# Gate and up projections of a decoder trunk by one level of Strassen's algorithm

## The chip, the cores and the metric

The kernel runs on one NeuronCore of a Trainium2 chip, which has a matrix engine (TensorE, PE in the rows; PEld is its weight load), three engines for elementwise work (VectorE = DVE, ScalarE = ACT, GpSimd = POOL) and a queue for loads (SyncE = SP). The metric is the device time of one execution, in microseconds (us), and the median over runs.

## What is computed

Two layers, each a half-weighted SwiGLU feed-forward, a mixer of three attentions, and a second feed-forward, on 512 tokens of width 1024. The change touches the feed-forwards alone: four of them, with 2816 hidden columns.

```python
def swiglu(h, w_gate, w_up, w_down):
    return (jax.nn.silu(h @ w_gate) * (h @ w_up)) @ w_down

for layer in range(DEPTH):                       # DEPTH = 2
    x = x + 0.5 * swiglu(rmsnorm(x, norm_g[layer, 0]), ffn_w_gate[layer, 0], ffn_w_up[layer, 0], ffn_w_down[layer, 0])
    x = x + hybrid_mixer(rmsnorm(x, norm_g[layer, 1]), ...)
    x = x + 0.5 * swiglu(rmsnorm(x, norm_g[layer, 2]), ffn_w_gate[layer, 1], ffn_w_up[layer, 1], ffn_w_down[layer, 1])
```

## The kernel before

Everything is float32. x lies transposed: the 1024 channels on the partitions in 8 chunks of 128, the 512 tokens along the columns. Each operand of a product is split into a high part (ScalarE copies it into the matrix engine's rounded float32) and a low part (VectorE subtracts the high part), and `mm3` makes one product of three matrix instructions: high by low, high by high, low by high. The norm's gain is applied before the products, 1/rms per token (`n.rb`, broadcast over the partitions) afterwards.

A feed-forward goes through its 22 hidden chunks of 128 in three parts (`FF_PARTS`: 8, 8 and 6 chunks). For each chunk `f`, two weight tiles of 128x1024 (gate and up) are loaded on SP's queue and split by `load_w`; 8 products for gate go into a bank of PSUM, 8 for up into another, 512 columns each, 48 matrix instructions in all. `activated` then makes silu(gate) * up: VectorE scales the gate by `rb`, ScalarE takes silu, GpSimd scales by `rb` once more, VectorE multiplies by up, and the result is split again into `h` and `lo`. When a part's chunks are done, its share of the down projection follows: 8 chunks of x, each with one weight tile and 3 instructions per hidden chunk, added to x.

The buffers that matter: `RAW = 4` raw weight tiles, `HL = 4` high and low parts of them, three banks each with the tags `sc` and `tr` and two with `mm`. A scheduler sets the order of instructions on every engine when the program is built; each engine then works through its own list strictly in that order and waits on semaphores where an operand isn't ready. Within the matrix engine's list the chunks of a part follow one another.

Of the kernel before, what the change touches and what calls it, by code (L numbers as in the profile page):

```python
# [22 lines left out]
T = 512          # tokens  # L23
NT = T // P      # token tiles
D = 1024
KD = D // P      # chunks of the model width
DFF = 2816
NF = DFF // P    # chunks of the feed-forward width
# [3 lines left out]
TOPK = 128       # min(256, 512 // 4)  # L32
NEG = -1e30
TAKEN = -3e38
WCOLS = 1024     # columns of one weight tile
SLOTS = 35       # buffers of [P, 512] for hidden chunks, x, heads and outputs
T1 = 3           # buffers by tag
# [4 lines left out]
RAW = 4  # L42
HL = 4
BANKS = {"mm": 2, "sc": 3, "tr": 3}
WARM = 9         # products of zeros at the start
# attention beside the dense products, counted in steps of six of these
RATE = 1         # units of attention per step
PICKS = 0.36     # rounds of the top-k per step
LAG_I, LAG_N = 4, 7             # from a projection to the split of its heads, without and with their norm
LAG_S, LAG_H = 4, 3             # to the norm's scaling; from the split to the transposes  # L50
LAG_T, LAG_C, LAG_V = 3, 5, 2   # from the softmax to the transposes (C: with both its maps), to the values
AHEAD = 4        # gates of branch a that come before its attention's end
FF_PARTS = [(0, 8), (8, 8), (16, 6)]
# [5 lines left out]
# columns of w_in, as the reference splits them  # L59
# [16 lines left out]
def trunk_kernel(ctx, tc, xt_in, pos_in, ng_in, wgu, wdn, wgrp, wgate, wbr_s, wbr_c, wo, qkg_in, lam_in, subg_in, out):  # L76
# [6 lines left out]
    tmp = ctx.enter_context(tc.tile_pool(name="tmp", bufs=2))  # L83
    sm = ctx.enter_context(tc.tile_pool(name="sm", bufs=3))
# [12 lines left out]
    def slot(dt=F32, tag="h", cols=512):  # L97
        return big.tile([P, cols], dt, tag=tag, name=nm(tag), bufs={"h": SLOTS, "xs": 16}[tag])

    def temp(tag, dt=F32, cols=512, bufs=2):  # L100
        return tmp.tile([P, cols], dt, tag=tag, name=nm(tag), bufs=bufs)

    # products of zeros, while the first loads are under way, bring the array's clock up
# [19 lines left out]
    causal = const.tile([P, 512], BF16, name="causal")   # last 128 columns: 0 on and below the diagonal  # L123
# [170 lines left out]
    def ffn(l, half, n, nxt, aside=None, x_src=None):  # L294
        for pi, (f0, nf) in enumerate(FF_PARTS):
            hh, hl = [], []
            late = []
            for f in range(f0, f0 + nf):
# [4 lines left out]
                if first:  # L303
                    for c in range(1, KD):
                        n.chunk(c, x_from(x_src, c), False)
# [572 lines left out]
```

## Time and profile before

| | |
|---|---|
| median of 3 runs | 2357.59 us (2356.71 to 2360.36) |
| profiled execution: span from first to last instruction | 2354.5 us |
| what lies around the span, by the median | 3.1 us |
| PE busy | 2338.9 us, 99% of the span |
| DVE, ACT, POOL busy | 1251.1, 897.3, 476.8 us |
| granted TensorE clock, mean | 0.999 |

The span is what the trace shows; the profiled execution's own device time is not listed apart from it, so the runs' median stands beside it. The page's busy time of an engine counts the time in which it had work in hand, so 99% for PE says that it hardly ever had none, not that each product runs at its best. The other engines' idle time costs nothing as long as PE doesn't wait for them.

### The profile page before, as it was taken

The numbers are of one execution on the slowest core, as the hardware profiler recorded it, in microseconds if no ns is written. First come the engines' busy times: TensorE is split into PE (matmuls) and PEld (weight loads), VectorE is DVE, ScalarE is ACT, GpSimd is POOL, SyncE is SP. The second block draws the span as 40 slices with busy tenths as digits, with TensorE's granted clock in tenths as the row PEclk, the third lists the DMA queues.
The fourth block names the chain that finished last, engine by engine and source line by source line (L and its number), as shares of the span: only waits on it lengthen the run. The fifth ranks groups of instructions, "written<-read, shape, count | busy, mean of one in ns | idle before, by whom it ended". The sixth has DMA issues, their size and how long they took to land.

```text
span 2354.5 us, 29137 instructions
## 1 busy us (share of the span) xinstructions
PE 2338.9 (99%) x11077; PEld 1939.2 (82%) x11077; DVE 1251.1 (53%) x2244; ACT 897.3 (38%) x1634; POOL 476.8 (20%) x495
## 2 busy tenths in 40 slices
PE   9999999999999999999999999999999999999999
PEld 7888888888888888888888888888888888888887
DVE  5434344788865543333443343447889665433333
ACT  4322234666534432222332222346755343322221
POOL 3101013454111310110220110134641112101010
PEclk9999999999999999999999999999999999999999
DMA  5333333323222333333333333332322223333332
GB/s 170 110 99 99 96 97 99 104 79 93 81 94 81 129 96 99 97 94 95 98 101 93 95 99 99 108 112 78 95 77 81 91 85 125 99 98 99 99 92 69
DMA packets 71290, 229.64 MB, mean 98 GB/s; under 512 B 8688, under 2 KB 8688, under 8 KB 71152
## 3 DMA queue, kind: packets, MB, share of 16 engines
q1 hardware_dynamic: 70432, 227.12, 31.2%
q8 instruction: 87, 1.43, 0.2%
q10 hardware_dynamic: 720, 0.68, 0.1%
q14 instruction: 51, 0.42, 0.1%
HBM read 214.13 MB, written 6.29 MB: 94 GB/s over the span
## 4 chain that ended last, share of the span: by engine, by line
PE 93%; DVE 3%; DMA 1%; POOL 1%; issue 1%; ACT 0%; SPq 0%; POOLq 0%; ACTq 0%; DVEq 0%
PE mm L214 18%; PE mm L216 17%; PE mm L215 17%; PE sc L214 8%; PE sc L215 8%; PE sc L216 8%; PE mm L364 4%; PE mm L365 4%; PE mm L366 4%; DMA h<-h 1%; PE sc L453 1%; PE sc L454 1%; PE tr L476 1%; PE tr L435 1%; PE tr L501 1%
## 5 line engine op out<-in xcount | busy, mean ns | idle before, releaser
L208 ACT ACTIVATE hi<-raw 128x1024 fp32r<-128x1024 f32 (+3 forms) x410 | 421.8, 1030 | 1118.6 <-PE mm L215 719.2
L209 DVE TENSOR_TENSOR lo<-raw,hi 128x1024 fp32r<-128x1024 f32 (+3 forms) x410 | 500.6, 1222 | 74.5 <-ACT hi L208 73.5
L214 PE MATMUL mm<-xs,hi 128*128 128x512 f32 x1088 | 431.2, 396 | 1.2 <-DVE xs L232 1.2
L216 PE MATMUL mm<-xs,lo 128*128 128x512 f32 x1088 | 425.0, 391 | 0.0
L215 PE MATMUL mm<-xs,hi 128*128 128x512 f32 x1088 | 424.9, 390 | 0.0
L282 POOL TENSOR_TENSOR t<-t,rb 128x512 f32<-128x512 f32 x88 | 149.2, 1696 | 1110.9 <-ACT t L281 1110.9
L214 PE MATMUL mm<-h,hi 128*128 128x512 f32 x832 | 324.1, 390 | 0.5 <-DVE h L805 0.5
L216 PE MATMUL mm<-h,lo 128*128 128x512 f32 x832 | 323.7, 389 | 0.0
L215 PE MATMUL mm<-h,hi 128*128 128x512 f32 x832 | 323.7, 389 | 0.0
L214 PE MATMUL sc<-xs,hi 128*128 128x512 f32 x704 | 274.7, 390 | 1.3 <-ACT hi L208 1.3
L216 PE MATMUL sc<-xs,lo 128*128 128x512 f32 x704 | 274.3, 390 | 0.0
L215 PE MATMUL sc<-xs,hi 128*128 128x512 f32 x704 | 274.1, 389 | 0.0
L214 PEld LDWEIGHTS mm<-xs,hi 128*128 128x128 f32 x1088 | 204.6, 188 | 44.1 <-issue 2.4
L216 PEld LDWEIGHTS mm<-xs,lo 128*128 128x128 f32 x1088 | 204.7, 188 | 43.1
L215 PEld LDWEIGHTS mm<-xs,hi 128*128 128x128 f32 x1088 | 205.0, 188 | 39.0
L284 DVE TENSOR_TENSOR t<-sc,t 128x512 f32<-128x512 f32 x88 | 60.9, 692 | 286.6 <-PE sc L216 277.2
L329 DVE SCALAR_TENSOR_TENSOR h<-mm,h 128x512 f32<-128x512 f32 x96 | 66.4, 692 | 264.1 <-PE mm L216 264.1
L214 PEld LDWEIGHTS mm<-h,hi 128*128 128x128 f32 x832 | 156.2, 188 | 34.2 <-DVE h L805 2.0
L215 PEld LDWEIGHTS mm<-h,hi 128*128 128x128 f32 x832 | 156.2, 188 | 32.4
L216 PEld LDWEIGHTS mm<-h,lo 128*128 128x128 f32 x832 | 156.2, 188 | 32.3
L279 DVE TENSOR_TENSOR t<-mm,rb 128x512 f32<-128x512 f32 x88 | 60.7, 691 | 220.8 <-PE mm L216 220.8
L364 PE MATMUL mm<-hi,xs 128*128 128x512 f32 (+2 forms) x448 | 172.3, 385 | 0.0
(293 smaller groups left out, 3166.7 us busy)
## 6 DMA issues: line engine op xcount, KB each, us to landing
raw<-in_wgu SPq DMA_DIRECT2D x174, 512.0 KB, 3.6
raw<-in_wdn SPq DMA_DIRECT2D x64, 512.0 KB, 3.5
raw<-in_wgate SPq DMA_DIRECT2D x48, 512.0 KB, 3.6
raw<-in_wgrp SPq DMA_DIRECT2D x40, 512.0 KB, 3.6
raw<-in_wdn SPq DMA_DIRECT2D x32, 384.0 KB, 3.1
raw<-in_wo SPq DMA_DIRECT2D x16, 512.0 KB, 3.5
h<-h SPq DMA_DIRECT2D x56, 128.0 KB, 4.4
aside<-h SPq DMA_DIRECT2D x16, 256.0 KB, 2.0
```

The source lines that it names most:

```text
L208: S.activation(hi[:, sl], raw[:, sl], AF.Copy)
L209: V.tensor_tensor(lo[:, sl], raw[:, sl], hi[:, sl].bitcast(F32), op=ALU.subtract)
L214: PE.matmul(o, ah, bl, start=first, stop=False)
L215: PE.matmul(o, ah, bh, start=False, stop=False)
L216: return PE.matmul(o, al, bh, start=False, stop=last)
L279: V.tensor_tensor(g, pg, n.rb, op=ALU.mult)
L282: G.tensor_tensor(s, s, n.rb, op=ALU.mult)
L284: V.tensor_tensor(hf, pu, s, op=ALU.mult)
L329: V.scalar_tensor_tensor(x[d], o, 0.5, x[d], op0=ALU.mult, op1=ALU.add)
L364: PE.matmul(o[:, :w_cols], xl, wh[:, sl], start=k == 0, stop=False)
L365: PE.matmul(o[:, :w_cols], xh, wh[:, sl], start=False, stop=False)
L366: last_dense[0] = PE.matmul(o[:, :w_cols], xh, wl[:, sl], start=False, stop=k == KD - 1)
```

## The change

Tokens are halved into a left and a right half of 256 columns, the model chunks into even and odd ones, and the outputs of a chunk into gate and up. The eight half-size products of these halves (2 by 2 by 2) become seven, by one level of Strassen's algorithm in a form with 15 sums. In short:

- **x** (`fold`): for each pair of an even and an odd chunk, VectorE, GpSimd and ScalarE make the halves, their sums and differences, and both parts of each, 256 columns wide. This happens when x is finished (at the start, or as the stage before ends).
- **weights** (`folded_w`): two raw tiles `r0`, `r1` per hidden chunk. The two parts of `r0` as before, 1024 wide (weights 1 and 2). GpSimd makes four sums, 128x512 each: `s1`, `s3` in new buffers (`SUMS = 3`), two in place over raw halves. Then ScalarE and VectorE split five tiles of 128x512 (`shi`, `slo`; `SHL = 5`) for weights 6, 5, 7, 3 and 4.
- **products** (`gate_up`): seven products of 4 x 3 matrix instructions, 256 columns each, in the order 1, 2, 6, 5, 7, 3, 4, on two banks: the left half of one (`sc`, called `q`) gathers products 1, 6, 7, 4, the other (`tr`, called `o`) 2, 5, 3. In between, ScalarE copies what `q` holds after product 1 and after product 6 (the two halves of `e`, below eL and eR), and what `o` holds on the right after product 5 (`u`); VectorE adds to `u` after product 7, and `o` to `e` after product 3. A product that goes on in `q` waits for the copy or sum that reads it.
- **`activated`**: as before, with the two halves of `hf` made apart, and with -1/rms (`nrb`) on GpSimd.
- parts of 6, 6, 5 and 5 chunks in place of 8, 8 and 6; one pool of 48 buffers in place of 35 and 16; a pool per stage, for the tiles that only one stage needs; a new layout of the gate and up weights.

The diff, cut to its core:

```diff
-SLOTS = 35
+SLOTS = 48
+SUMS = 3
+SHL = 5
-FF_PARTS = [(0, 8), (8, 8), (16, 6)]
+FF_PARTS = [(0, 6), (6, 6), (12, 5), (17, 5)]
+H2 = T // 2
+Q4 = KD // 2
...
+        def fold(self, c, xc):
+            g = ng[:, self.idx * KD + c:self.idx * KD + c + 1]
+            L, R = slice(0, H2), slice(H2, T)
+            if c % 2 == 0:
+                bh, bl = slot(F32R), slot(F32R)
+                y = temp("t2")
+                V.tensor_scalar(y, xc, g, None, op0=ALU.mult)
+                d = temp("t0", cols=H2)
+                S.activation(bh[:, L], y[:, L], AF.Copy)
+                G.tensor_tensor(d, y[:, L], y[:, R], op=ALU.subtract)
+                V.tensor_tensor(bl[:, L], y[:, L], bh[:, L].bitcast(F32), op=ALU.subtract)
+                S.activation(bh[:, R], d, AF.Copy)
+                V.tensor_tensor(bl[:, R], d, bh[:, R].bitcast(F32), op=ALU.subtract)
...
+                return
+            y, d = self.even
+            ah, al = slot(F32R), slot(F32R)
+            S.activation(ah, xc, AF.Copy, scale=g)
+            V.scalar_tensor_tensor(al, xc, g, ah.bitcast(F32), op0=ALU.mult, op1=ALU.subtract)
...
+            V.scalar_tensor_tensor(f[:, R], xc[:, R], g, d, op0=ALU.mult, op1=ALU.add)
+            V.scalar_tensor_tensor(f[:, L], xc[:, R], g, y[:, R], op0=ALU.mult, op1=ALU.subtract)
...
+            S.activation(ch[:, R], f[:, R], AF.Copy, scale=-1.0)
+            V.scalar_tensor_tensor(cl[:, R], f[:, R], -1.0, ch[:, R].bitcast(F32), op0=ALU.mult, op1=ALU.subtract)
+            S.activation(ch[:, L], f[:, L], AF.Copy)
+            V.tensor_tensor(cl[:, L], f[:, L], ch[:, L].bitcast(F32), op=ALU.subtract)
...
+            V.scalar_tensor_tensor(q, xc[:, L], g, f[:, R], op0=ALU.mult, op1=ALU.subtract)
+            S.activation(dh, q, AF.Copy, scale=-1.0)
+            V.scalar_tensor_tensor(dl, q, -1.0, dh.bitcast(F32), op0=ALU.mult, op1=ALU.subtract)
...
+    def folded_w(src, pieces=1):
+        r0, r1 = (wp.tile([P, WCOLS], F32, tag="raw", name=nm("raw"), bufs=RAW) for _ in range(2))
+        L, R = slice(0, 512), slice(512, 1024)
+        h0, l0 = (wp.tile([P, WCOLS], F32R, tag=t, name=nm(t), bufs=HL) for t in ("hi", "lo"))
...
+            nc.sync.dma_start(r0, src[0])
+            S.activation(h0, r0, AF.Copy)
+            V.tensor_tensor(l0, r0, h0.bitcast(F32), op=ALU.subtract)
+        nc.sync.dma_start(r1, src[1])
+        pool = phase[-1]
+        s1, s3 = (pool.tile([P, 512], F32, tag="sum", name=nm("sum"), bufs=SUMS) for _ in range(2))
+        G.tensor_tensor(s1, r1[:, L], r1[:, R], op=ALU.add)
+        G.tensor_tensor(s3, r0[:, R], r1[:, L], op=ALU.add)
+        G.tensor_tensor(r1[:, L], r0[:, R], s1, op=ALU.add)
+        G.tensor_tensor(r0[:, R], r0[:, L], r1[:, L], op=ALU.add)
+        w = {1: (h0[:, R], l0[:, R]), 2: (h0[:, L], l0[:, L])}
+        for j, t in ((6, r1[:, L]), (5, s1), (7, s3), (3, r0[:, R]), (4, r1[:, R])):
+            h, lo = (pool.tile([P, 512], F32R, tag=x, name=nm(x), bufs=SHL) for x in ("shi", "slo"))
+            S.activation(h, t, AF.Copy)
+            V.tensor_tensor(lo, t, h.bitcast(F32), op=ALU.subtract)
+            w[j] = h, lo
+        return w
+
+    def gate_up(n, w, after):
+        q, o = bank("sc"), bank("tr")
+        L, R = slice(0, H2), slice(H2, T)
+        def product(j, to, first):
+            for i in range(Q4):
+                (ah, al), (bh, bl) = (x[:, i * P:(i + 1) * P] for x in w[j]), n.ops[j][i]
+                mm = mm3(to, ah, al, bh, bl, first and i == 0, i == Q4 - 1, not first)
+            after(mm)
+        e = temp("e")
+        product(1, q[:, L], True)
+        product(2, o[:, L], True)
+        S.activation(e[:, L], q[:, L], AF.Copy)
+        product(6, q[:, L], False)
+        product(5, o[:, R], True)
+        S.activation(e[:, R], q[:, L], AF.Copy)
+        u = temp("u", cols=H2)
+        S.activation(u, o[:, R], AF.Copy)
+        product(7, q[:, L], False)
+        product(3, o[:, R], False)
+        V.tensor_tensor(u, q[:, L], u, op=ALU.add)
+        V.tensor_tensor(e, e, o, op=ALU.add)
+        product(4, q[:, L], False)
+        return e, q[:, L], u
+
+    def activated(n, e, q, u):
+        L, R = slice(0, H2), slice(H2, T)
+        V.tensor_tensor(e, e, n.rb, op=ALU.mult)
         s = temp("t1", bufs=T1)
-        S.activation(s, g, AF.Silu)
-        G.tensor_tensor(s, s, n.rb, op=ALU.mult)
+        S.activation(s, e, AF.Silu)
+        G.tensor_tensor(s, s, n.nrb, op=ALU.mult)
         hf = temp("t2")
-        V.tensor_tensor(hf, pu, s, op=ALU.mult)
+        V.tensor_tensor(hf[:, L], q, s[:, L], op=ALU.mult)
+        V.tensor_tensor(hf[:, R], u, s[:, R], op=ALU.mult)
...
-                ws = [load_w(wgu[l, half, f, j], WCOLS, 2 if first else 1) for j in range(2)]
+                w = folded_w(wgu[l, half, f], 2 if first else 1)
...
+                late.append(gate_up(n, w, n.advance))
```

How the order moves, at three places of the first feed-forward, in the middle of a part. First ACT's list. Before, in the part's fourth to sixth chunk (L208 is the high part of a raw tile, L281 silu, L286 the high part of the result):

```order
L208 ACTIVATE hi_657<-raw_656 128x1024
L281 ACTIVATE t_107_574<-t_106_572 128x512
L208 ACTIVATE hi_663<-raw_662 128x1024
L286 ACTIVATE h_579<-t_108_577 128x512
L208 ACTIVATE hi_730<-raw_729 128x1024
L281 ACTIVATE t_120_647<-t_119_645 128x512
L208 ACTIVATE hi_736<-raw_735 128x1024
L286 ACTIVATE h_652<-t_121_650 128x512
```

And of the change, around its second part's second chunk, whose banks are `sc_1553` and `tr_1554` (the first one's are 1415 and 1416; L392 is eL, L416 the high part `h` of the chunk before, L360 the 1024-wide high part h0 of the part's fourth chunk, L372 the high parts of the third chunk's folded weights, L395 eR, L397 the copy u):

```order
L392 ACTIVATE e_1555<-sc_1553 128x256
L416 ACTIVATE h_1515<-t_272_1512 128x512
L360 ACTIVATE hi_1797<-raw_1795 128x1024
L372 ACTIVATE shi_1671<-raw_1658 128x512
L395 ACTIVATE e_1555<-sc_1553 128x256
L372 ACTIVATE shi_1675<-sum_1665 128x512
L397 ACTIVATE u_1606<-tr_1554 128x256
L372 ACTIVATE shi_1679<-sum_1666 128x512
L372 ACTIVATE shi_1683<-raw_1657 128x512
L372 ACTIVATE shi_1687<-raw_1658 128x512
```

Two high parts and two steps of the activation a chunk have become three copies out of PSUM, six high parts and two steps, and the copies stand between them: eR behind `h`, h0 and a `shi`. Next DVE's list. Before (L279 and L284 multiply out of PSUM, L209 is a low part, L287 the result's):

```order
L279 TENSOR_TENSOR t_106_572<-mm_522,rb_340 128x512
L209 TENSOR_TENSOR lo_658<-raw_656,hi_657 128x1024
L284 TENSOR_TENSOR t_108_577<-sc_523,t_107_574 128x512
L209 TENSOR_TENSOR lo_664<-raw_662,hi_663 128x1024
L287 TENSOR_TENSOR h_580<-t_108_577,h_579 128x512
L279 TENSOR_TENSOR t_119_645<-mm_595,rb_340 128x512
```

And of the change, from the low part l0 of the fourth chunk to the end of the second one's activation (L373 are low parts of the third chunk's folded weights, L400 adds to u, L401 adds o to e, L408 is e by rb, L413 and L414 the halves of hf, L417 the result's low part):

```order
L361 TENSOR_TENSOR lo_1798<-raw_1795,hi_1797 128x1024
L373 TENSOR_TENSOR slo_1672<-raw_1658,shi_1671 128x512
L373 TENSOR_TENSOR slo_1676<-sum_1665,shi_1675 128x512
L400 TENSOR_TENSOR u_1606<-sc_1553,u_1606 128x256
L373 TENSOR_TENSOR slo_1680<-sum_1666,shi_1679 128x512
L401 TENSOR_TENSOR e_1555<-e_1555,tr_1554 128x512
L373 TENSOR_TENSOR slo_1684<-raw_1657,shi_1683 128x512
L408 TENSOR_TENSOR e_1555<-e_1555,rb_524 128x512
L373 TENSOR_TENSOR slo_1688<-raw_1658,shi_1687 128x512
L413 TENSOR_TENSOR t_296_1650<-sc_1553,t_295_1647 128x256
L414 TENSOR_TENSOR t_296_1650<-u_1606,t_295_1647 128x256
L417 TENSOR_TENSOR h_1654<-t_296_1650,h_1653 128x512
```

Five operations a chunk have become twelve, and u and e stand behind low parts of later weights. Last POOL's list. Before, one product a chunk (L282):

```order
L282 TENSOR_TENSOR t_94_501<-t_94_501,rb_340 128x512
L282 TENSOR_TENSOR t_107_574<-t_107_574,rb_340 128x512
L282 TENSOR_TENSOR t_120_647<-t_120_647,rb_340 128x512
L282 TENSOR_TENSOR t_133_720<-t_133_720,rb_340 128x512
L282 TENSOR_TENSOR t_146_793<-t_146_793,rb_340 128x512
```

And of the change (L411 is the product with nrb, of the first and the second chunk; L365 to L368 are the four sums of the fourth and, at the end, the fifth):

```order
L411 TENSOR_TENSOR t_271_1509<-t_271_1509,nrb_526 128x512
L365 TENSOR_TENSOR sum_1803<-raw_1796 128x512
L366 TENSOR_TENSOR sum_1804<-raw_1795,raw_1796 128x512
L367 TENSOR_TENSOR raw_1796<-raw_1795,sum_1803 128x512
L368 TENSOR_TENSOR raw_1795<-raw_1795,raw_1796 128x512
L411 TENSOR_TENSOR t_295_1647<-t_295_1647,nrb_526 128x512
L365 TENSOR_TENSOR sum_1941<-raw_1934 128x512
```

The four sums of the chunk after next have come between one chunk's product and the next one's.

## Rows read from the trace of the kernel before

**Rows 1.** The page: busy time by engine; the chain that ended last, by engine.
```profile
PE 2338.9 (99%) x11077; PEld 1939.2 (82%) x11077; DVE 1251.1 (53%) x2244; ACT 897.3 (38%) x1634; POOL 476.8 (20%) x495
...
PE 93%; DVE 3%; DMA 1%; POOL 1%; issue 1%; ACT 0%; SPq 0%; POOLq 0%; ACTq 0%; DVEq 0%
```

**Rows 2.** Windows, gate/up then down: length; PE, PEld, DVE, ACT, POOL busy; clock; DMA.
```profile
952.06:1039.10 87.04, 87.04 (x385) 72.07 (x384) 34.89 (x39) 25.11 (x31) 14.28 (x8) 1.00 0.32 97
1039.10:1082.62 43.52, 43.52 (x193) 36.04 (x192) 15.94 (x17) 9.07 (x10) 0.00 (x0) 1.00 0.32 97
```

**Rows 3.** Timeline of PE: start, duration, what; attention scores (L453, L454).
```profile
501.77 0.28 PE L453 MATMUL sc<-h,h 128*128 128x256 f32 x1
501.89 0.28 PE L454 MATMUL sc<-h,h 128*128 128x256 f32 x1
502.01 0.34 PE L364 MATMUL mm<-hi,xs 128*128 128x384 f32 x1
```

**Rows 4.** Groups by line and shape: count, busy us, mean ns, idle before.
```profile
L209 DVE TENSOR_TENSOR lo<-raw,hi 128x1024 fp32r<-128x1024 f32 x358 | 450.9, 1260 | 67.0 <-ACT hi L208 66.3
L287 DVE TENSOR_TENSOR h<-t,h 128x512 fp32r<-128x512 f32 x88 | 62.5, 710 | 1.5 <-ACT h L286 1.4
...
L232 DVE SCALAR_TENSOR_TENSOR xs<-h,ng,xs 128x512 fp32r<-128x512 f32 x48 | 38.4, 804 | 3.6 <-ACT xs L231 3.6
...
L463 DVE CUSTOM_DVE_ANT_0 p<-sc,causal 128x256 f32<-128x256 f32 x24 | 10.0, 415 | 0.0
...
L655 DVE SCALAR_TENSOR_TENSOR p<-p,f,p 128x256 f32<-128x256 f32 x8 | 4.2, 530 | 0.1
...
L208 ACT ACTIVATE hi<-raw 128x1024 fp32r<-128x1024 f32 x358 | 379.4, 1061 | 1013.6 <-PE mm L215 669.1 <-PE sc L215 281.7 <-issue 50.4
L286 ACT ACTIVATE h<-t 128x512 fp32r<-128x512 f32 x88 | 55.6, 632 | 10.8 <-DVE t L284 5.0 <-DVE invf L169 4.8
L208 ACT ACTIVATE hi<-raw 128x768 fp32r<-128x768 f32 x40 | 33.8, 846 | 100.1 <-PE mm L215 50.1 <-PE sc L215 30.7 <-issue 17.4
...
L592 ACT ACTIVATE t<-sc 128x256 f32<-128x256 f32 x16 | 5.9, 382 | 4.0 <-PE sc L454 2.2 <-DVE ss L392 1.3 <-DVE h L593 0.4
```

**Rows 5.** Timelines of ACT and DVE around one chunk's end.
```profile
1006.48 1.06 ACT L208 ACTIVATE hi<-raw 128x1024 fp32r<-128x1024 f32 x1 [3.85 <-PE sc L215]
1007.46 0.63 ACT L286 ACTIVATE h<-t 128x512 fp32r<-128x512 f32 x1
...
1007.57 1.23 DVE L209 TENSOR_TENSOR lo<-raw,hi 128x1024 fp32r<-128x1024 f32 x1 [0.15 <-ACT hi L208]
1008.72 0.69 DVE L287 TENSOR_TENSOR h<-t,h 128x512 fp32r<-128x512 f32 x1
```

**Rows 6.** Timelines of DVE and POOL where both are at work, two places.
```profile
671.78 2.33 DVE L209 TENSOR_TENSOR lo<-raw,hi 128x1024 fp32r<-128x1024 f32 x1
671.75 1.28 POOL L726 TENSOR_TENSOR h<-h,t 128x512 f32<-128x512 f32 x1 [6.87 <-DVE t L725]
...
840.08 1.78 DVE L287 TENSOR_TENSOR h<-t,h 128x512 fp32r<-128x512 f32 x1
840.02 1.28 POOL L282 TENSOR_TENSOR t<-t,rb 128x512 f32<-128x512 f32 x1 [3.22 <-ACT t L281]
```

**Rows 7.** Single lines: count, then duration in ns, least/median/most.
```profile
L284 DVE TENSOR_TENSOR t<-sc,t x88: 691/692/692, 38.2 to 2318.1; 128x512 f32<-128x512 f32 x88
L287 DVE TENSOR_TENSOR h<-t,h x88: 681/686/1780, 40.1 to 2319.6; 128x512 fp32r<-128x512 f32 x88
L282 POOL TENSOR_TENSOR t<-t,rb x88: 1284/1790/1811, 36.9 to 2314.1; 128x512 f32<-128x512 f32 x88
```

**Rows 8.** Loads: issuer, count, size each, median us from issue to landing.
```profile
raw<-in_wgu SPq DMA_DIRECT2D x174, 512.0 KB, 3.6
```

**Rows 9.** The start: a wait of PE (timeline), then a window as in rows 2.
```profile
10.35 0.79 PE L214 MATMUL mm<-xs,hi 128*128 128x512 f32 x1 [0.94 <-DVE xs L232]
9.90:13.40 3.50, 3.05 (x7) 2.47 (x8) 3.21 (x7) 3.50 (x7) 0.00 (x0) 0.51 1.05 410
```

## What I expect, before the run

> **What bounds the kernel now.** First the busy times: the matrix engine (PE) is busy in 99% of a span of 2354.5 us, and the chain that ended last is PE for 93% [rows 1]. So the time is the number of products times their spacing. Then a stretch of one kind: in one feed-forward part, 8 chunks of gate and up take 87.04 us, which is 10.88 us a chunk of 48 products, 0.227 us each; its 192 down products take 43.52 us, the same spacing. In that stretch DVE works 34.89 us of 87.04 and POOL 14.28 [rows 2]: both have room, and that room is what the change spends.
>
> **What it removes: PE time.** A chunk (there are 22 in each of 4 feed-forwards, 88) goes from 48 products of 512 columns to 84 of 256, each with its own weight load. The only 256-column rows are the attention scores: three products start 0.12 us apart, each behind a new weight load [rows 3]. I take 0.118 (between 0.115 and 0.12 as the starts are rounded): 84 × 0.118 = 9.91 us. A fixed cost shows here: half the columns cost more than half of 0.227. Gain: 88 × (10.88 − 9.91) = **85 us**, if PE never waits. [...]
>
> **What it adds, per chunk.** DVE: the low parts of one 1024-wide and five 512-wide tiles (1.26 and 0.71 us), three 512-wide operations on e and h (0.69 to 0.71), three of 256 (about 0.41): 8.3 us. ACT: 1.06 + 5 × 0.63 + 3 × 0.38 + 2 × 0.63 = 6.6 us. POOL: four sums and one product of 512, 1.28 us each when undisturbed: 6.4 us [rows 4, 7]. Each is under 9.91, so by busy shares all of it would hide. Two things say no.
>
> **The port.** DVE and POOL keep each other out. A POOL product of 1.28 us began 0.03 us before a low-part subtraction of DVE, which then took 2.33 instead of 1.22 us; another held a 0.69 us subtraction for 1.78 [rows 6]. POOL's own product, which mostly begins under a low part, has a median of 1.79 over a least of 1.28 [rows 7]. Operations of DVE with one operand in PSUM never lengthen (691 to 692 ns over 88), those with both in SBUF do (681 to 1780) [rows 7]. So it is one at a time, and of a waiting operation some 0.14 us are already behind it when the other ends: 0.55 us of 0.69 remain, 1.08 of 1.22, 1.15 of 1.28. The Trainium skill ("SBUF — State Buffer", section Who interferes with whom) states this rule, that two SBUF inputs on DVE and a POOL operation that reads SBUF exclude each other, and that the loser waits for the whole instruction. With full instructions for the remainders, the cycle below would be about 0.6 us longer and the sum, over 40 such chunks, some 22 us more; the rows' remainders are used. Before, the two met once a chunk, off the path; now DVE has nine such operations a chunk and POOL five.
>
> **The cycle.** Names are those of the order shown above. Let a chunk's product 1 start at 0; the due starts are then 1.42 (2), 2.83 (6), 4.25 (5), 5.66 (7), 7.08 (3), 8.50 (4), and its last result comes 0.16 after 9.91. In a part's first chunk everything lies ready: e is added at 8.72 to 9.41 (after product 3), one low part, e·rb until 10.64, silu until 11.37, and POOL's product with nrb starts at 11.44. Count on from that start (DVE and ACT pass from one operation to the next 0.08 us before its end, and 0.04 to 0.07 us pass between engines [rows 5]). POOL's product ends at 1.29, hf is done at 2.11, h at 2.83. On ACT there then stand, in this order, the high part of the chunk after next (until 3.80), shi of weight 6 (4.34) and only then the copy eR (4.63), for which product 7 waits: product 7 can start 4.70 after POOL's product. For the second chunk that is 11.44 + 4.70 = 16.14 against a due 9.91 + 5.66 = 15.57: a stall of 0.6 us.
>
> Now the sums. The raw tile of chunk c+2 reuses the buffer that chunk c gives back with its last low part, just before POOL's product with nrb, and lands 3.6 us later [rows 8]. So sum 1 begins at 3.65 and holds the port to 4.95; l0 of the same tile, ready at 3.87, ends at 6.03 instead of 5.10. Two low parts follow (to 7.25), then u, to 7.6; product 4 waits for it, starts at 7.67 and ends at 9.09. Sum 2 needs the buffer which the second of these low parts frees (three buffers, two in use): 7.3 to 8.6, so the next low part ends at 9.15; e follows until 9.8; sum 3 holds the port to 10.30, a low part ends at 10.85; sum 4 to 12.0, e·rb ends at 12.55, silu at 13.25: POOL's next product starts at **13.3**. Without the port the same cycle closes at 10.45. So a chunk costs 13.3 us while there are sums to make, where 10.88 stood before.
>
> **Counting chunks.** Sums are made inside a part only for its chunks 4 and later: in the second, third and fourth chunk of a part of six. The second still starts on time and pays 0.6 of stall and the wait for u: 10.6. In the last but one, two down tiles' high parts (0.85 each) take the place of l0's: 12.9. The last one has little left: 10.1. Part of six: 9.9 + 10.6 + 13.3 + 13.3 + 12.9 + 10.1 = 70.1, of five: 56.8, against 59.5 and 49.6 of bare products. There are 8 of each: stalls 8 × 10.6 + 8 × 7.2 = **+142 us**.
>
> **The other terms.** Part ends: from the last product, hf, h and its low part take 4.6 us; PE has 16 down products (3.63 us) before it needs them: 1.0 × 16 = **+16** (bounds 0 and 30; down tiles of another size cost nothing, as their products are the same 2112). Folding x: two chunks of x cost DVE about 5.1 us instead of 1.6, by the 512-wide 0.80 and the 256-wide 0.53 and 0.41 [rows 4]; 14 us more for eight, of which 10 are exposed at the start, where PE already waits, and 3 at each of three later hand-overs, only the last pair showing: **+20** (bounds 5 and 40). The clock: at the start PE had little to do and waited again 0.94 us, and the granted clock of that stretch was 0.51, the 1.2 GHz level [rows 9]. Stalls before product 7 now reach 3.3 us, in 40 chunks. If each brings that level for the three products behind it, the cycle grows by 1.0: bounds 0 and 40, I take half, **+20**.
>
> Sum: −85 + 142 + 16 + 20 + 20 = +113. On the span of 2354.5 that is 2467.5; the median of the runs, 2357.59, lies 3.1 above the span, so **2471 us**.
>
> **The rivals.**
> - *The port is not met.* If the sums fall where DVE does PSUM work or waits, the cycle is 10.45: parts of 62.0 and 51.5 against 65.3 and 54.4 before, 16 of them −50, with +16 and +20: 2344. For it: DVE idles some 2 us a cycle, and a raw tile that lands later moves all four meetings. Against: with four sums in a row of operations that follow each other closely there is little room. It decides the sign: faster begins where these cycles fall under about 10.8 us (40 of them, 2.35 us below the 13.15 of the count, take back 94).
> - *It does what it says*: eR and u come in time, by slack that I miss: −85, +16 at the part ends: 2288. Against: the copy stands behind h on ACT, and h behind POOL.
> - *All later chunks are slow*: lateness doesn't end with the sums, so 72 chunks at 14: 16 × 9.9 + 72 × 14.0 − 957 = +209, +36: about 2600.
>
> **How the numbers follow.** Forecast 0.65, with its own range 2400 to 2540 (a cycle of 12 to 14.3); port not met 0.15; as it says 0.10; all slow 0.10. The range 2335 to 2560 leaves out the last two cases and little else. A measurement of this kernel tells 0.2% from no change, here 2352.9 and 2362.3: faster takes the 0.10 and two thirds of the 0.15, 0.20; the same 0.03; slower 0.77.
>
> **What would show it.** Products of 256 columns 0.118 apart inside a run; in the list of PE's waits the first product of weights 7 and 4 behind ACT's eR and DVE's u, some 100 us or more in all; POOL's sums and DVE's 512-wide low parts well over their undisturbed 1.28 and 0.69 in the chunks with sums; from one product with nrb to the next 13.3 us there, 10 to 11 in a part's last chunk. If eR is not waited for, or the low parts keep 0.69, the forecast is wrong at the cycle.

## The result: 2607.7 us, 10.6% slower

The changed kernel takes 2607.7 us (median of four runs, 2604.6 to 2611.7), against 2357.2 in the same session: ratio 1.106, 95% interval 1.1045 to 1.1077. The forecast had the direction and the loop behind it; its 2471 us is 137 us too low, and its range ended at 2560.

### The profile after

The page of the changed kernel, busy time by engine:

```profile
PE 2359.5 (91%) x14245; PEld 2070.7 (79%) x14245; DVE 1792.5 (69%) x3051; ACT 1164.3 (45%) x2349; POOL 969.2 (37%) x863
```

Beside [rows 1]: PE's share fell from 99 to 91%; DVE has 541 us more, POOL 492. Nobody but PE is near its limit, yet PE waits. For whom, PE's list of waits says (total us, times, longest):

```profile
PE sc L220 <- ACT e L395: 75.4, 58, 3.2
PE sc L220 <- ACT e L392: 63.3, 60, 1.8
PE mm L220 <- ACT hi L360: 25.3, 8, 3.3
PE mm L220 <- DVE h L942: 13.4, 4, 3.6
PE sc L220 <- DVE h L255: 13.1, 6, 6.5
PE mm L220 <- DVE h L417: 10.6, 15, 0.7
PE tr L220 <- DVE h L265: 8.4, 3, 7.7
...
PE sc L220 <- DVE u L400: 0.5, 2, 0.3
```

The first two lines are waits inside chunks, for eR (L395) and for eL (L392): 139 us. The forecast had named eR (product 7) and u (product 4), not eL (product 6); u is hardly waited for. The other lines lie outside what the forecast worked out: down products (mm behind L360, L417), the end of the mixers (L942), folding x (L255, L265).

Where the time lies, by windows of the second feed-forward: gate and up of the first part (6 chunks), its down products, gate and up of the second part (6), gate and up of the third (5), then the mixer (the attention stage) ahead of them. Columns as in [rows 2]; each stretch runs from its first matrix instruction, a weight load included, to the first of the next.

```profile
902.79:983.45 80.66, 67.77 (x514) 64.97 (x513) 63.34 (x82) 37.68 (x71) 36.99 (x24) 0.96 0.26 79
983.45:1023.69 40.24, 36.28 (x147) 28.92 (x146) 16.66 (x23) 10.43 (x14) 13.34 (x10) 0.92 0.27 79
1023.69:1095.93 72.24, 62.52 (x505) 60.57 (x504) 52.13 (x66) 32.11 (x60) 28.68 (x21) 1.00 0.29 88
...
1136.26:1194.60 58.34, 51.83 (x421) 50.41 (x420) 40.88 (x54) 25.83 (x49) 21.26 (x15) 1.00 0.27 82
...
439.48:902.79 463.31, 451.35 (x2347) 375.72 (x2346) 341.83 (x789) 240.20 (x568) 152.65 (x196) 0.99 0.30 89
```

Six chunks take 72.24 us (12.0 each) and five 58.34, where the forecast counted 70.1 and 56.8. But 144 down products take 40.2 us, where the spacing of [rows 2] makes 32.6 of them, and the mixer 463.3. Cut in this way, all stretches of a kernel and some 10 us before the first product and behind the last add up to its span. The whole document goes by this table (sums in us; "first parts" are gate and up of the first part of each feed-forward, "other parts" gate and up of the twelve that follow, "down products" those of all sixteen; the row of before is the kernel before cut into the same parts, an experiment below):

| kernel | time | first parts (4) | other parts (12) | down products (16) | mixers (2) |
|---|---|---|---|---|---|
| before, parts 6, 6, 5, 5 | 2357.9 | 272 | 696 | 478 | 898 |
| changed | 2607.7 | 359 | 765 | 547 | 925 |
| difference | +250 | +87 | +69 | +69 | +27 |
| forecast of it | +113 | +39 | +38 | +16 | 0 (20 for the clock unplaced) |

(The forecast's parts of 70.1 and 56.8 us against 65.3 and 54.4 of before are +38 over 4 and 8 parts and +19 over the four first ones, to which its 20 for folding are added.)

### The cycle, as forecast

A cycle is the time from one chunk's product with nrb (L411, on POOL) to the next chunk's. Timelines of POOL, then DVE, then ACT of the changed kernel for one cycle, from the product of a part's second chunk to that of its third:

```profile
1050.22 1.28 POOL L411 TENSOR_TENSOR t<-t,nrb 128x512 f32<-128x512 f32 x1 [1.35 <-ACT t L410]
1053.73 1.26 POOL L365 TENSOR_TENSOR sum<-raw 128x512 f32<-128x512 f32 x1 [2.22 <-DVE h L417]
1057.36 1.29 POOL L366 TENSOR_TENSOR sum<-raw,raw 128x512 f32<-128x512 f32 x1 [2.37 <-DVE slo L373]
1058.72 1.62 POOL L367 TENSOR_TENSOR raw<-raw,sum 128x512 f32<-128x512 f32 x1
1060.42 1.62 POOL L368 TENSOR_TENSOR raw<-raw,raw 128x512 f32<-128x512 f32 x1
1063.40 1.28 POOL L411 TENSOR_TENSOR t<-t,nrb 128x512 f32<-128x512 f32 x1 [1.35 <-ACT t L410]
...
1053.94 2.13 DVE L361 TENSOR_TENSOR lo<-raw,hi 128x1024 fp32r<-128x1024 f32 x1 [0.25 <-ACT hi L360]
...
1057.54 1.66 DVE L373 TENSOR_TENSOR slo<-sum,shi 128x512 fp32r<-128x512 f32 x1
...
1059.71 1.18 DVE L373 TENSOR_TENSOR slo<-raw,shi 128x512 fp32r<-128x512 f32 x1
1060.82 1.78 DVE L408 TENSOR_TENSOR e<-e,rb 128x512 f32<-128x512 f32 x1
...
1050.05 0.36 ACT L392 ACTIVATE e<-sc 128x256 f32<-128x256 f32 x1
1052.33 0.63 ACT L416 ACTIVATE h<-t 128x512 fp32r<-128x512 f32 x1 [1.92 <-DVE t L414]
1052.87 1.04 ACT L360 ACTIVATE hi<-raw 128x1024 fp32r<-128x1024 f32 x1
1053.82 0.61 ACT L372 ACTIVATE shi<-raw 128x512 fp32r<-128x512 f32 x1
1054.34 0.36 ACT L395 ACTIVATE e<-sc 128x256 f32<-128x256 f32 x1
```

Counted from POOL's start: h until 2.74 (forecast 2.83), eR until 4.48 (4.63), first sum at 3.51 (3.65), second at 7.14 (7.3), which waits for the buffer that a low part frees; the next product with nrb at **13.18 (13.3)**. Four of DVE's operations are held, one by each sum, as counted: l0 takes 2.13, two low parts 1.66 and 1.18, e by rb 1.78. And h, h0 and one shi stand ahead of eR on ACT. POOL itself stood idle for 1.35 us before its product, waiting for silu: its own list doesn't set the pace.

### The profile page after: what moved, and what is told of

Same layout as the page of the kernel before. It is cut to its first block, busy times and chain, and to the rows that moved or that the text cites. A ratio compares the mean times of both kernels' runs of the same rounds, so it can differ in the third digit from the quotient of the medians.

```text
span 2605.9 us, 37948 instructions
## 1 busy us (share of the span) xinstructions
PE 2359.5 (91%) x14245; PEld 2070.7 (79%) x14245; DVE 1792.5 (69%) x3051; ACT 1164.3 (45%) x2349; POOL 969.2 (37%) x863
## 5 line engine op out<-in xcount | busy, mean ns | idle before, releaser
L220 PE MATMUL mm<-h,hi 128*128 128x512 f32 x1216 | 495.2, 407 | 55.9 <-ACT hi L360 25.3
L221 PE MATMUL mm<-h,hi 128*128 128x512 f32 x1216 | 484.4, 398 | 0.0
L220 PE MATMUL sc<-h,shi 128*128 128x256 f32 x1056 | 317.0, 300 | 142.8 <-ACT e L395 75.4
L373 DVE TENSOR_TENSOR slo<-raw,shi 128x512 fp32r<-128x512 f32 x264 | 239.5, 911 | 168.5 <-ACT shi L372 168.3
L220 PEld LDWEIGHTS sc<-h,shi 128*128 128x128 f32 x1056 | 201.4, 191 | 172.5 <-ACT e L395 87.3
L213 ACT ACTIVATE hi<-raw 128x1024 fp32r<-128x1024 f32 (+3 forms) x264 | 238.7, 911 | 214.4 <-PE mm L221 178.1
L214 DVE TENSOR_TENSOR lo<-raw,hi 128x1024 fp32r<-128x1024 f32 (+3 forms) x264 | 288.4, 1098 | 30.5 <-ACT hi L213 29.4
L372 ACT ACTIVATE shi<-raw 128x512 fp32r<-128x512 f32 x264 | 163.6, 626 | 309.0 <-POOL raw L368 99.3
L222 PE MATMUL sc<-h,slo 128*128 128x256 f32 x1056 | 300.4, 284 | 0.0
L221 PE MATMUL sc<-h,shi 128*128 128x256 f32 x1056 | 299.4, 284 | 0.0
L365 POOL TENSOR_TENSOR sum<-raw 128x512 f32<-128x512 f32 x88 | 128.1, 1455 | 378.0 <-DMA raw<-in_wgu 340.4
L411 POOL TENSOR_TENSOR t<-t,nrb 128x512 f32<-128x512 f32 x88 | 118.8, 1351 | 351.5 <-ACT t L410 351.5
L221 PEld LDWEIGHTS sc<-h,shi 128*128 128x128 f32 x1056 | 202.0, 191 | 0.0
L222 PEld LDWEIGHTS sc<-h,slo 128*128 128x128 f32 x1056 | 202.0, 191 | 0.0
L220 PE MATMUL tr<-h,shi 128*128 128x256 f32 x704 | 201.4, 286 | 0.1
L221 PE MATMUL tr<-h,shi 128*128 128x256 f32 x704 | 201.0, 286 | 0.0
L222 PE MATMUL tr<-h,slo 128*128 128x256 f32 x704 | 200.1, 284 | 0.0
L373 DVE TENSOR_TENSOR slo<-sum,shi 128x512 fp32r<-128x512 f32 x176 | 167.8, 956 | 17.0 <-ACT shi L372 15.1
```

Source lines behind the costliest of these rows:

```text
L213: S.activation(hi[:, sl], raw[:, sl], AF.Copy)
L214: V.tensor_tensor(lo[:, sl], raw[:, sl], hi[:, sl].bitcast(F32), op=ALU.subtract)
L220: PE.matmul(o, ah, bl, start=first, stop=False, skip_group_check=onto)
L221: PE.matmul(o, ah, bh, start=False, stop=False, skip_group_check=onto)
L222: last_mm[0] = PE.matmul(o, al, bh, start=False, stop=last, skip_group_check=onto)
L365: G.tensor_tensor(s1, r1[:, L], r1[:, R], op=ALU.add)
```

## The experiments

In the table, the columns are those above; each row is a kernel with one edit of the changed one, or with several where it says so.

| kernel | time | first parts | other parts | down | mixers |
|---|---|---|---|---|---|
| changed | 2607.7 | 359 | 765 | 547 | 925 |
| no sums | 2377.0 | 300 | 665 | 497 | 905 |
| sums made, unread | 2560.6 | 365 | 741 | 522 | 917 |
| sums on VectorE | 2421.6 | 314 | 688 | 498 | 910 |
| h behind eR | 2562.3 | 347 | 733 | 547 | 924 |
| 1/rms late | 2556.9 | 342 | 722 | 544 | 937 |
| last splits behind down products | 2591.9 | 359 | 791 | 505 | 926 |
| weights of a part's first chunk reused | 2350.8 | 280 | 640 | 506 | 913 |
| three edits | 2367.3 | 295 | 655 | 486 | 918 |
| three edits, plain x | 2344.8 | 279 | 659 | 482 | 914 |
| the same, chunks dealt otherwise | 2344.2 | 280 | 660 | 482 | 914 |
| three edits, folding shared | 2395.6 | 307 | 655 | 489 | 930 |

### No sums

```diff
-        G.tensor_tensor(s1, r1[:, L], r1[:, R], op=ALU.add)
...
-        for j, t in ((6, r1[:, L]), (5, s1), (7, s3), (3, r0[:, R]), (4, r1[:, R])):
+        for j, t in ((6, r1[:, L]), (5, r0[:, L]), (7, r1[:, R]), (3, r0[:, R]), (4, r1[:, R])):
```

> Leaves out GpSimd's four weight sums (raw halves are split in their place, so the products are other ones; all other work stays). Theory A (the count: sums on the port between DVE and POOL lengthen a loop that goes over POOL's product with nrb, h and the copy eR): 10.5 us a chunk in place of 13.2, parts of 62 and 52 us in place of 72.4 and 58.8, so 8 x 10.4 + 8 x 6.8 = 138 less; of the waits in the down products, which stand behind splits of sums, some 30 to 45 go too: 2425 to 2470 us. Rival B (the copies out of PSUM between products of one chunk hold PE whatever POOL does): above 2560. Rival C (loads into four raw buffers set the pace): loads are the same, so above 2560.

2377.0 us, ratio 1.008 (1.0066 to 1.0096): below all theories. The cycle is 10.4 us, as theory A counted; six chunks of the same part as above take 62.25 us. B and C fall: neither the copies nor the loads account for the loss. What A missed is the size: the four sums cost 231 us, of which 100 lie in the other parts, 59 in the first ones, 50 in the down products and 20 in the mixers. Windows of the down products and of the second part:

```profile
907.16:940.84 33.68, 32.95 (x147) 27.00 (x146) 17.02 (x23) 10.56 (x14) 1.29 (x1) 1.00 0.30 94
940.84:1003.09 62.25, 61.20 (x504) 60.19 (x503) 41.12 (x66) 32.81 (x60) 6.46 (x5) 1.00 0.34 102
```

### Sums on VectorE

```diff
-        G.tensor_tensor(s1, r1[:, L], r1[:, R], op=ALU.add)
+        V.tensor_tensor(s1, r1[:, L], r1[:, R], op=ALU.add)
```

(and the other three likewise)

> The four weight sums on VectorE instead of GpSimd, 0.69 us each, so DVE has 2.8 us more a chunk (8.3 + 2.8 = 11.1) but meets POOL only at its one product with nrb. Theory A: the sums cost 2.8 where they and what they held up cost about 5, so the cycle falls from 13.2 to about 12 us: 2510 to 2570. If the port costs nothing and DVE's place in line decides: DVE is the longer by 2.8 in every cycle, 16 us a chunk with sums, above 2650.

2421.6 us, ratio 1.027 (1.0252 to 1.0283). The same sums, on the engine that was already the busier one, cost 45 us over none at all, where on GpSimd they cost 231. The direction is A's, the size well beyond it: the cycle is 11.2 to 11.4, not 12, and the down products are nearly free again (33.7 us in place of 40.2). The second part, by windows:

```profile
954.16:1018.30 64.14, 61.53 (x505) 60.25 (x503) 49.19 (x83) 32.24 (x60) 7.71 (x5) 1.00 0.34 99
```

and DVE's low parts in it, by groups of one line (count, busy us and mean ns, idle before):

```profile
L373 DVE TENSOR_TENSOR slo<-raw,shi 128x512 fp32r<-128x512 f32 x15 | 10.2, 686 | 4.1 <-ACT shi L372 4.1
L373 DVE TENSOR_TENSOR slo<-sum,shi 128x512 fp32r<-128x512 f32 x10 | 6.8, 684 | 0.7 <-ACT shi L372 0.7
```

DVE now does 83 operations there instead of 66 in less time (49.19 against 52.13 us): its low parts take 0.69 again.

### Sums made, but unread

```diff
-        G.tensor_tensor(r1[:, L], r0[:, R], s1, op=ALU.add)
-        G.tensor_tensor(r0[:, R], r0[:, L], r1[:, L], op=ALU.add)
+        G.tensor_tensor(s5, r0[:, R], r1[:, R], op=ALU.add)
+        G.tensor_tensor(s7, r0[:, L], r1[:, L], op=ALU.add)
```

(into new tiles; the splits as in the kernel without sums)

> GpSimd makes its four sums of the same sizes out of the same raw tiles, but into tiles that nobody reads; the splits take raw halves, as in the kernel without sums (other products, same work). Theory A1 (the port: POOL's sums hold up DVE's operations wherever they fall): DVE's 512-wide low parts and e by rb stay lengthened, the cycle stays at 12.3 to 13.2 us, 2510 to 2600 us. Rival F (the chain load, four sums one after the other, split: ACT and DVE stand in line behind a split whose sum isn't there yet): without a reader of the sums the cycle is the 10.4 of the kernel without sums, waits in the down products go, 2375 to 2420 us. In between: the share of each.

2560.6 us: of the 231 us, 184 stay although nobody waits for a sum, and the cycle is 13.2 again in the middle of a part. So theory A1 holds for four fifths, the chain of rival F has the rest (47). By stages the shares differ: all 59 us of the first parts stay (365 against 359 with the sums read), 76 of 100 in the other parts, but only 25 of 50 in the down products and 12 of 20 in the mixers. Two other ways in which unread sums could cost time are not seen: SP's list of waits names no operation of GpSimd, so that the loads were not held by the sums, and GpSimd stands idle for 1.98 us, waiting for silu, before the product with nrb of a cycle with sums. The same stretch, DVE's low parts in the changed kernel:

```profile
L373 DVE TENSOR_TENSOR slo<-raw,shi 128x512 fp32r<-128x512 f32 x15 | 12.2, 816 | 4.1 <-ACT shi L372 4.1
L373 DVE TENSOR_TENSOR slo<-sum,shi 128x512 fp32r<-128x512 f32 x10 | 10.2, 1022 | 0.8 <-ACT shi L372 0.7
```

and with unread sums, followed by two of POOL's groups:

```profile
L373 DVE TENSOR_TENSOR slo<-raw,shi 128x512 fp32r<-128x512 f32 x25 | 27.1, 1096 | 5.1 <-ACT shi L372 4.9
...
L366 POOL TENSOR_TENSOR sum<-raw,raw 128x512 f32<-128x512 f32 x4 | 7.5, 1868 | 0.0
...
L367 POOL TENSOR_TENSOR sum<-raw,raw 128x512 f32<-128x512 f32 x4 | 6.5, 1613 | 0.0
```

Both sides are held: 1.10 us for 0.69, and 1.6 to 1.9 for 1.28. An operation of DVE with an operand in PSUM is not held in the changed kernel either (count, least/median/most ns), where e by rb, with both in SBUF, is held most times:

```profile
L400 DVE TENSOR_TENSOR u<-sc,u x88: 407/418/427, 43.5 to 2571.2; 128x256 f32<-128x256 f32 x88
...
L408 DVE TENSOR_TENSOR e<-e,rb x88: 678/1776/1785, 64.0 to 2573.3; 128x512 f32<-128x512 f32 x88
```

The Trainium skill ("Perfetto Trace Analysis", section Optimizing Scalar/DVE Operations) says that moving work between VectorE and GpSimd may not help because they share a port; the two runs agree, 2421.6 against 2607.7 us.

### h behind eR

```diff
-        S.activation(e[:, R], q[:, L], AF.Copy)
+        er = S.activation(e[:, R], q[:, L], AF.Copy)
+        if waiting:
+            with behind(er.ins):
+                waiting.pop(0)()
```

> The split of a chunk's result (ACT's h, DVE's low part) is moved behind the next chunk's copy eR on ACT; all work and all sums stay. Theory A (loop over POOL's product, h, eR): product 7 no longer waits for POOL's product, its waits of 1.3 us go (75 us in all in the changed kernel), and what is left is the time the port is held by both, 11.7 to 12.9 a chunk: 2530 to 2580. Rival D (only the work on the port sets the pace, not the order on ACT): the waits move to another product, 2600 to 2615. Rival E (only the order does): 10.5 a chunk, 2470.

2562.3 us: A's range. The cycle falls from 13.2 to 12.4. The waits of product 7 (L397 here) shrink, those of product 6 (L394) hardly do, and those of product 4 (L405) grow:

```profile
PE sc L220 <- ACT e L394: 61.6, 53, 1.8
...
PE sc L220 <- ACT e L397: 21.4, 20, 3.2
PE sc L220 <- DVE u L405: 14.3, 31, 0.6
```

So of 13.2 us about 0.8 is the order on ACT, and 12.4 what the port and the rest of the loop ask. D and E fall.

### 1/rms late

```diff
-        G.tensor_tensor(s, s, n.nrb, op=ALU.mult)
...
-                V.scalar_tensor_tensor(x[d], o, 0.5, x[d], op0=ALU.mult, op1=ALU.add)
+                y = temp("t2")
+                V.tensor_tensor(y, o, n.nrb, op=ALU.mult)
+                V.scalar_tensor_tensor(x[d], y, 0.5, x[d], op0=ALU.mult, op1=ALU.add)
```

> The second scaling by 1/rms is taken out of the chunks (POOL's product with nrb is gone) and done on the down products, on DVE out of PSUM, 8 more operations of 0.69 us a part. Theory A: the loop loses 1.35 us of POOL and one meeting of 1.1, 13.2 to about 11.5 a chunk: 2490 to 2540. If the loop doesn't go over this product: 2600 or, by the added DVE work in the down products, slower.

2556.9 us: the loop does go over this product, but only 1.2 us of 13.2 go (12.0 a chunk), less than its own 1.35, and the mixers get 12 us longer. The expectation was 17 us too low or more: the meeting on the port that is taken out there is made at other places. In this run the low parts of the second part take longer, 0.97 and 1.13 us on the mean, where the changed kernel (shown above) has 0.82 and 1.02:

```profile
L373 DVE TENSOR_TENSOR slo<-raw,shi 128x512 fp32r<-128x512 f32 x15 | 14.5, 966 | 3.4 <-ACT shi L372 3.4
```

### Last splits behind the down products

```diff
-            S.activation(h, t, AF.Copy)
-            V.tensor_tensor(lo, t, h.bitcast(F32), op=ALU.subtract)
+            with behind(last_mm[0].ins) if late and j in (3, 4) else nullcontext():
+                S.activation(h, t, AF.Copy)
+                V.tensor_tensor(lo, t, h.bitcast(F32), op=ALU.subtract)
```

> The changed kernel, with the last two splits (weights 3 and 4) of a part's first chunk put behind the part before's last down product, so that no addition to x on DVE stands behind a split that waits for GpSimd's sums. Nothing is left out. Theory G (PE waits in the down products for a bank, which such an addition frees, which stands behind a split): the 3.3 us waits before the last down tile (25 in all) and the stretch of half clock behind them (some 2 to 3 us each) go, down products of a six-chunk part 38 to 40 to about 34 us: 2560 to 2580 us. Rival H (the weights come too late whatever the order): the wait moves to the next part's first chunk, 2595 to 2610.

What it is about, in the changed kernel: timelines of SP, POOL, ACT, DVE and PE in the down products of a first part, up to the last down tile.

```profile
1006.02 0.33 SPq L362 DMA_DIRECT2D raw<-in_wgu  x1
...
1009.68 1.29 POOL L365 TENSOR_TENSOR sum<-raw 128x512 f32<-128x512 f32 x1 [7.15 <-DMA raw<-in_wgu]
...
1013.54 1.26 POOL L368 TENSOR_TENSOR raw<-raw,raw 128x512 f32<-128x512 f32 x1
...
1014.83 1.15 ACT L372 ACTIVATE shi<-raw 128x512 fp32r<-128x512 f32 x2 [8.68 <-POOL raw L368]
...
1015.50 0.69 DVE L373 TENSOR_TENSOR slo<-raw,shi 128x512 fp32r<-128x512 f32 x1 [7.17 <-ACT shi L372]
1016.10 0.68 DVE L456 SCALAR_TENSOR_TENSOR h<-mm,h 128x512 f32<-128x512 f32 x1
...
1016.93 0.77 PE L220 MATMUL mm<-h,hi 128*128 128x512 f32 x1 [3.24 <-ACT hi L360]
```

and the window behind that wait:

```profile
1016.70:1022.80 6.10, 5.87 (x14) 4.65 (x15) 3.59 (x5) 1.28 (x2) 2.02 (x2) 0.50 0.54 173
```

A raw tile of the next part lands, POOL needs 5.1 us for its four sums, ACT stands in line behind the split of one, DVE behind ACT, and behind that low part stands the addition to x (L456) that frees PE's bank. It ends at 1016.78, and PE goes on at 1016.93; the profile names L360, the high part of a tile of the next part, which this product doesn't read and which ended last. PE has waited 3.24 us, and then runs 14 products at a granted clock of 0.50, its lower level (1.2 GHz). (PE's list has eight such waits; behind the one that ends at 1440.55 the clock stays at 1.00, as a line in the last section shows.) Together some 6 of the 7.6 us that these down products have too much. (The Trainium skill, "PSUM — Partial Sum Buffer", section Engine vs sequencer instructions, has it that the queues of ScalarE, VectorE and GpSimd are strictly first in, first out; this is what that looks like.)

The edit changes only the order. The same down products, by windows, then the part that follows them:

```profile
981.17:1015.11 33.94, 33.24 (x147) 26.93 (x146) 14.58 (x20) 9.49 (x13) 12.78 (x9) 1.00 0.20 62
1015.11:1090.32 75.21, 63.20 (x504) 60.69 (x503) 55.78 (x69) 32.93 (x61) 30.66 (x21) 1.00 0.32 99
```

33.94 us at clock 1.00: theory G, in place and size (42 us over the kernel). But the next part takes 75.21 instead of 72.24, 26 us over the kernel, as rival H said of where the work would go. Net 16 us, 2591.9: above G's range (2580) and 3 us below H's (2595). Each holds for its half.

### Weights reused; parts alone

```diff
-                w = folded_w(wgu[l, half, f], 2 if first else 1)
+                if f == f0:
+                    w = folded_w(wgu[l, half, f], 2 if first else 1)
```

> The weights of a part's first chunk serve all its chunks: 22 - 4 of 22 loads, sums and splits of a feed-forward are left out (other products); folding x, the copies out of PSUM, the activation and the shorter parts stay. It shows what matrix work, folding and part ends give without weight work: if product spacing is 0.119 as in the trace, a chunk takes 10.0 us, 77 less in all than before; part ends 16 x 1 and the exposed folding some 30 to 50 come on top: 2310 to 2350 us. If the copies between products hold PE by themselves, a chunk is over 10.4 and the time above 2360.

2350.8 us, ratio 0.997 (0.9964 to 0.9983), at the upper end of the first range. The second part by windows:

```profile
930.01:989.97 59.96, 59.96 (x505) 59.91 (x504) 20.23 (x36) 14.81 (x30) 6.45 (x5) 1.00 0.06 17
```

9.99 us a chunk: the gain in matrix work is 88 x (10.88 - 9.99) = 78 us, where the forecast said 85. But all but 7 of it is used up elsewhere, although only one chunk in a part has its weights split: against the kernel before in the same parts, the first parts have 8 us more instead of 20 less, the down products 28 more, the mixers 15.

For the kernel before, one line: `FF_PARTS = [(0, 6), (6, 6), (12, 5), (17, 5)]`.

> The kernel before with parts of 6, 6, 5 and 5 chunks and nothing else. The count of the change took four more part ends of 1.0 us each as the price of all part ends (16); in the kernel before, whose chunks end early enough, a part end costs PE nothing: 2355 to 2362 us. If shorter parts cost loads or waits of their own: above 2370.

2357.9 us, ratio 1.0005 (0.9995 to 1.0014): the parts by themselves cost nothing.

### Three edits together

Sums on VectorE, 1/rms late and h behind eR.

> The changed kernel with weight sums on VectorE, the second 1/rms on the down products and the chunk's result split behind the next copy eR, all three together. GpSimd has no work in the chunks, so nothing is held on the port. Theory A: what is left is DVE's own work, 8.3 + 2.8 = 11.1 us a chunk, a little over the 10.88 of the kernel before: 2390 to 2420 us. If the three edits took away the same waits: no better than sums on VectorE alone, 2421 us.

2367.3 us, ratio 1.004 (1.0023 to 1.0052): better than expected, and still not as good as the kernel before. 240 us of the 250 are gone. My 11.1 us of DVE a chunk were no bound: a chunk takes 10.1 (60.68 for six), since part of the splitting is done during down products, where DVE has room.

```profile
903.34:935.99 32.65, 32.65 (x147) 27.07 (x146) 26.07 (x39) 10.44 (x14) 0.00 (x0) 1.00 0.31 97
935.99:996.67 60.68, 60.66 (x505) 60.17 (x504) 49.49 (x83) 32.13 (x60) 0.00 (x0) 1.00 0.33 105
```

In these stretches PE has no wait left, but 41 us gained in the other parts (655 against 696) are given back in first parts (23), mixers (20) and down products (8).

### What folding x costs

On top of the three edits: x not folded (each chunk split once, halves of it as operands); the same with the first four chunks of x for products 1, 2 and 6; and the folding kept, with its sums on GpSimd and ScalarE.

```diff
-                V.tensor_scalar(y, xc, g, None, op0=ALU.mult)
...
-                G.tensor_tensor(d, y[:, L], y[:, R], op=ALU.subtract)
...
             S.activation(ah, xc, AF.Copy, scale=g)
             V.scalar_tensor_tensor(al, xc, g, ah.bitcast(F32), op0=ALU.mult, op1=ALU.subtract)
...
+            a, b = (ah[:, L], al[:, L]), (ah[:, R], al[:, R])
```

> The kernel with all three edits (weight sums on VectorE, second 1/rms on the down products, result split behind eR), and x not folded: only the two parts of each chunk are made, as before the change, and halves of them serve as operands of the seven products (other products, the same number). The count of the prediction put 20 us on folding. If folding is what the first part of each feed-forward and the mixers have too much in the trace (first parts 294.7 us in all, where 4 x 61 + 11 would be the like of other parts; 459 between feed-forwards where 449 stood): 40 and 20 less, 2305 to 2320 us. If 20 is the size of it: 2340 to 2350. If those places are long for another reason: above 2355.

2344.8 us: 22.5 less. The second reading holds: folding costs about the 20 of the forecast here, on top of the three edits. But the first parts stay long (279, where four like the other parts of six, 61.3 each, and the 11 by which the kernel before exceeds four times 65.3 make 256), and so do the mixers (914).

> The kernel with the three edits and x not folded, with the operands dealt out otherwise: products 1, 2 and 6 take halves of the first four chunks of x, products 5, 7, 3 and 4 of the last four (other products, the same number and work). So far product 1 needs all even chunks of x and product 2, 1.4 us later, all odd ones; in the kernel before the last chunk of x was wanted 4.8 us after the first. Theory J (first parts are long since the first products want all of x at once): the wait of 7.1 us at the start shrinks by 5 or more, each hand-over gains up to 2.8: first parts 278.9 down by 10 to 18, 2325 to 2336 us. Rival K (the splits and weights of the first chunk are late whatever the order of x): 2340 to 2350.

2344.2 us: nothing changed, J falls. At the start PE still waits once for 6.8 us, now for the first four chunks of x.

```diff
-            V.scalar_tensor_tensor(f[:, R], xc[:, R], g, d, op0=ALU.mult, op1=ALU.add)
...
+            G.tensor_tensor(f[:, R], yo[:, R], d, op=ALU.add)
```

> The kernel with all three edits, and the sums of the folding moved off VectorE: the gain by ScalarE (one more copy a pair), the three 256-wide sums by GpSimd; DVE has about 2.4 us a pair less of 5.1, GpSimd some 2.2 more. If DVE's time is what the folding costs: 10 to 20 us less than with the three edits, 2345 to 2358, level with the kernel before. If the port hands POOL's time on to DVE: 2362 to 2385.

2395.6 us, 28 more than with the folding on DVE: first parts and mixers, where the folding is, each 12 longer, beyond even the second reading. Work taken from DVE to POOL made it slower once more; whether by the port or by the longer way from engine to engine was not told apart here.

## Why the prediction missed

**Right.** The forecast had the loop to a tenth of a microsecond: over POOL's product, h, eR and the port, 13.3 us counted and 13.2 measured, 10.45 and 10.4 without the sums. It had a chunk's matrix work at 9.91 (9.99, so the gain is 78 us, not 85), the folding at 20 (22.5), and the part ends at 16: without sums the down products have 18.6 us more than before (497.0 against 478.4). Two slips changed nothing: the terms of DVE's 8.3 us a chunk add up to 8.1 or 8.2, and between ACT and DVE [rows 5] show 0.03 us, not 0.04.

**Wrong: "Counting chunks" and "Sums are made inside a part only for its chunks 4 and later".** The count charged the sums only where they lengthen this cycle: by its own cycles with and without the port, 8 x 8.1 + 8 x 5.3 = 107 us, of which 75 in the other parts and 32 in the first ones. They cost 231: 100 and 59 there. And in the stretches ahead of a part, to which the count gave no price, the sums of the next part's first chunks are made too. In the down products they cost 50 us: in the wait shown, an addition stands behind a low part that waits for a sum, and PE's granted clock is at 0.50 afterwards; half of the 50 stays with unread sums. At the end of the mixers they cost 20, where the additions (L942) wait in the same way. In first parts sums and folding are on the same two engines; with unread sums all of the 59 stays, but why it is 59 where 32 were counted is not shown.

**Sizes.** In the parts that are not a feed-forward's first: +69 us instead of +38. By the starts of its products the second chunk, counted at 10.6, already takes 12.2 to 13.5 (in the part shown it waits 0.50 us for eL and 1.17 for eR). The last but one takes 13.1 in a part of six and 12.9, as counted, in one of five. Product 6's wait for eL, behind silu on ACT, was not foreseen, and product 4's wait for u, which was, is hardly there (0.5 us in all); neither lies on the path that sets the cycle, since eR stands behind h on ACT anyway. The clock was counted at 20 of at most 40, and for the waits in chunks. In the second and third part shown it stayed at 1.00; it fell in the first part (0.96 in its window), in the down products (0.92) and at the ends of mixers (0.99 over the whole mixer shown).

**The rivals.** "The port is not met" and "It does what it says" are out. "All later chunks are slow", about 2600, is near the result by its number alone: the cycles are 13.2 and not 14, and a part's last chunk does recover (10.1 to 10.6 us by the starts of its products).

**Left open.** Some 23 us in first parts and 16 in mixers stay even without folding and sums; waits for x and for the first chunk's weights are seen there, but no run took them apart. The shares of port and chain were told apart in one way only, by sums that nobody reads.

## What to carry to other kernels

Busy shares don't price work that is given to a helper engine: ask whom each operation excludes, and who stands in line behind the first one that waits for it, in every stage in which the helper works ahead, not only in the one where its result is used. Where two engines keep each other out, as VectorE and GpSimd do here, try the faster one first even when it is the busier: the four sums cost 45 us on VectorE and 231 on GpSimd. And a saving in matrix work is worth no more than the stretches around it let through: with 78 us less matrix work the best form of this change that was tried is 0.4% slower than before.

## What was not expected of the hardware

Sums that nobody reads cost four fifths of those that are waited for: 184 of 231 us. Holding on the port lengthens both sides (DVE's 0.69 to 1.78, POOL's 1.28 to 1.87), so it counts twice in a loop that passes through both engines. Behind the wait of 3.24 us shown in the down products the granted clock stood at 0.50 for 14 products; in the second part's chunks, with waits of some 1.2 and 1.4 us in three of six, it stayed at 1.00. Behind a wait of 3.1 us before another last down tile it stayed at 1.00 too:

```profile
1440.30:1446.40 6.10, 5.85 (x32) 5.15 (x33) 4.26 (x6) 1.34 (x3) 2.04 (x2) 1.00 0.48 172
```
